# Turning sixteen pairs of gate-and-up results by DMA transposes of 16-bit halves

## The chip, the cores and the metric

The kernel runs on one core of one Trainium2 chip. The metric is the device time of one execution in microseconds (us).

## The reference

A decoder trunk of two layers on x of 512 tokens by 1024, in float32. Each layer has three parts, with a last norm behind the second layer:

```
x = x + 0.5 * swiglu(rms_norm(x, ffn1_norm), wg, wu, wd)      # D_FF = 2816
h = rms_norm(x, mix_norm); z = h @ w_in                       # q, k, v and three conv inputs
x = x + concat([sliding-window attention, short convolution]) @ w_out
x = x + 0.5 * swiglu(rms_norm(x, ffn2_norm), wg, wu, wd)

def swiglu(h, w_gate, w_up, w_down):
    return (jax.nn.silu(h @ w_gate) * (h @ w_up)) @ w_down
```

The change is in swiglu, of which there are four: between the product of gate and up, and the matmul with w_down.

## The kernel before

Every operand of a matmul is split into two parts, a rounded one (`h`, high) and the rest (`l`, low), and a product is three matmuls: high by high, low by high, high by low. The weights come from memory in tiles `raw` of 512 KB, which SyncE (SP) loads (`load`); some tiles are added to another by a second DMA that GpSimd (POOL) issues. ScalarE (ACT) casts a tile to `wh` and VectorE (DVE) subtracts, giving `wl` (`split`). There are three buffers each for `wh` and `wl`, and `take_split` splits two groups ahead (SPLIT_AHEAD = 2) of the group that TensorE (PE) works on.

Products of 2 x 2 blocks take seven block products in place of eight, after Strassen and Winograd; the sums of blocks have the names b11, b21, t2, t3, t1, t4, b22 (CHAINS). So a stage has seven steps, and each step two groups of 12 matmuls in `winograd2`. The class `Seven` makes the sums and their splits (`make`).

The 2816 columns of a feed-forward part are 22 columns of 128, in eleven pairs numbered 0 to 10. A list of stages says how they are worked (FIRST for the first part, INNER for the next two, LAST for the fourth):

```
FIRST = (
    ("p", 0), ("p", 1), ("d", (0,)), ("w", 2), ("d", (1,)), ("w", 4), ("w", 6), ("w", 8), ("u", 10),
    ("s", 2), ("d", (10,)), ("s", 6),
)
INNER = (
    ("p", 0), ("d", (0,)), ("w", 1), ("w", 3), ("w", 5), ("w", 7), ("w", 9), ("s", 1), ("s", 5),
    ("d", (9, 10)),
)
```

"w" with b computes gate and up for pairs b and b + 1 together (`winograd2`); what the change and the prediction call a pair is one such block of four columns. Its result lies with tokens on the partitions: four tiles `ups[t]` of 128 tokens by 512 columns. "s" with b multiplies the results of blocks b and b + 2 with w_down in seven products (`share`), and "d" does a plain product with w_down. Both need the results with columns on the partitions, so they have to be turned.

Before, `turn` does it: for each of the four columns c, four PE transposes of 128 x 128 into a PSUM tile `at` (line 1050), and one ACT copy of 128 x 512 from there into `raw_a` (line 1057, for blocks that go to an "s" stage) or a split (for those that go to "d"). The turns of a block wait in the list `pending`, and `turns(step)`, which the next stage calls after each of its steps, does one after steps 0 and 1 and two after step 2. A "d" stage does one after each column. There are 19 such blocks: sixteen go to "s" (`blocks`: four in each of the four parts), the rest are block 9 of INNER, twice, and of LAST, once.

`raw_a` is read when the operands of the "s" stage are made, which begins in the last stage ahead of it (in step 0 to 3 of "u" 10 or "w" 9).

The order in which instructions stand on an engine's queue is made by a scheduler when the kernel is built, from the program's order and its own estimate of when things are ready; each engine then works its queue strictly in that order. Buffers come from pools: `g2` (14 of 2 KB a partition), `g8` (4 of 8 KB), `xf` (`form`, 14 of 4 KB).

Of the kernel before, what the change touches and what calls it, by code (L numbers as in the profile page):

```python
# [8 lines left out]
F32 = mybir.dt.float32  # L9
F32R = mybir.dt.float32r  # L10
BF16 = mybir.dt.bfloat16
I32 = mybir.dt.int32
AF = mybir.ActivationFunctionType
ALU = mybir.AluOpType

P = 128
D = 1024
S = 512
# [5 lines left out]
KC = D // P  # L24
NT = S // P
# [46 lines left out]
def trunk_kernel(  # L72
# [23 lines left out]
    nc = tc.nc  # L96
# [8 lines left out]
    def psum(tag, shape, name):  # L105
        return ps.tile(shape, F32, tag=tag, bufs={"mm": 4, "sc": 2, "aux": 2}[tag], name=name)

    def g2(name, dt=F32, shape=(P, S)):
        return work.tile(list(shape), dt, tag="g2", bufs=14, name=name)

    def g8(name, dt=F32R, shape=(P, 2, 2, S)):
        return work.tile(list(shape), dt, tag="g8", bufs=4, name=name)
# [9 lines left out]
    def form(name, dt=F32R, shape=(P, KC // 2, H)):  # L122
        return xpool.tile(list(shape), dt, tag="xf", bufs=14, name=name)
# [7 lines left out]

    zero = const.tile([P, S], BF16, name="zero")
    nc.vector.memset(zero, 0.0)
# [311 lines left out]
    class Norm:  # L445
        def __init__(self, i):
            self.i = i
            self.h = [None] * KC
            self.acc = None
            self.inv = None  # L450
            self.pairs = {}
            self.begun = set()
            self.order = range(KC)
# [319 lines left out]
    bias_f = const.tile([P, NH * P], F32, name="bias")  # L773
    bias = bias_f.bitcast(BF16).rearrange("p (h k) -> p h k", h=NH)

    def make_bias():
        di = g2("dist_i", I32, (P, 2 * P))
        nc.gpsimd.iota(di, pattern=[[-1, 2 * P]], base=P, channel_multiplier=1)
        df = g2("dist", F32, (P, 2 * P))
        nc.vector.tensor_copy(df, di)  # L780
        m0 = g2("mask0", F32, (P, 2 * P))
        m1 = g2("mask1", F32, (P, 2 * P))
        nc.vector.tensor_scalar(m0, df, 0.0, FAR, op0=ALU.is_lt, op1=ALU.mult)
        nc.vector.tensor_scalar(m1, df, float(P), FAR, op0=ALU.is_ge, op1=ALU.mult)
        nc.vector.tensor_add(m0, m0, m1)
        for h in range(NH):
            nc.vector.scalar_tensor_tensor(
                bias[:, h, :], df, -(2.0 ** -(h + 1)), m0, op0=ALU.mult, op1=ALU.add
            )
# [99 lines left out]
    def ffn(norm, stages, after=None, late=None):  # L889
# [102 lines left out]
        def winograd2(b, between=None):  # L992


            name = f"{norm.i}_{b}"
            accs = {}
            gates = [g2(f"gate_{name}_{t}") for t in range(NT)]
            ups = [None] * NT
            kept = {}

            def keep(what, u, src):
                kept[what, u] = g2(f"{what}_{name}_{u}")
                nc.scalar.copy(kept[what, u], src)

            for step, (acc, operand, start) in enumerate(CHAINS):
                norm.make(operand)
                xh, xl = norm.forms[operand]
                if start:
                    tag = {"x": "mm", "y": "sc", "w": "aux"}[acc]
                    accs[acc] = [psum(tag, [P, S], f"{acc}_{name}_{u}") for u in range(2)]  # L1010
                for h in range(2):
                    _, wh, wl = take_split()
                    stream(accs[acc], wh, wl, xh, xl, h, start)
                    for u in range(2):
                        out = accs[acc][u]
                        if h == 0:
                            continue
                        if step == 0:
                            keep("p1", u, out)
                        if step == 1:  # L1020
                            nc.vector.tensor_add(gates[u], out, kept["p1", u])
                            nc.scalar.activation(gates[u], gates[u], AF.Silu)
                        if step == 2:
                            keep("u2", u, out)
                        if step == 3:
                            keep("p7", u, out)
                        if step == 4:
                            ups[2 + u] = kept["p7", u]
                            nc.vector.tensor_sub(ups[2 + u], ups[2 + u], out)
                        if step == 5:  # L1030
                            ups[u] = kept["u2", u]
                            nc.vector.tensor_sub(ups[u], out, ups[u])
                            nc.vector.tensor_mul(ups[u], ups[u], gates[u])
                        if step == 6:
                            nc.scalar.activation(gates[2 + u], out, AF.Silu)
                            nc.vector.tensor_mul(ups[2 + u], ups[2 + u], gates[2 + u])
                turns(step)
                if not first and step < 3:
                    norm.make(CHAINS[step + 4][1])
                if between:  # L1040
                    between(step)
            if b in blocks:
                raws[b] = g8(f"raw_a_{name}", F32, (P, KC // 2, S))
            if b in few:
                raws[b] = [form(f"raw_a{n}_{name}", F32, (P, 2, S)) for n in range(2)]

            def turn(c, tag="sc"):
                tp = psum(tag, [P, S], f"at_{name}_{c}")
                for t in range(NT):
                    nc.tensor.transpose(  # L1050
                        tp[:, t * P : (t + 1) * P], ups[t][:, c * P : (c + 1) * P], ident
                    )
                if b in few:
                    nc.scalar.copy(raws[b][c // 2][:, c % 2, :], tp)
                    return
                if b in raws:
                    nc.scalar.copy(raws[b][:, c, :], tp)
                    return
                if b + c // 2 not in acts:
                    acts[b + c // 2] = [form(f"a{n}_{name}_{c}", shape=(P, 2, S)) for n in "hl"]  # L1060
                hi, lo = acts[b + c // 2]
                split(hi[:, c % 2, :], lo[:, c % 2, :], tp)

            pending.extend(lambda *tag, c=c: turn(c, *tag) for c in range(NT))

        def shared(b):
            return Seven([raws[b], raws[b + 2]], room_form, f"s_{norm.i}_{b}")

        def turns(step):

            if step < 2:
                flush()
            if step == 2:
                flush(2, "mm")

        sevens = [b for what, b in stages if what == "s"]
        blocks = [b + j for what, b in stages if what in "se" for j in (0, 2)]
        few = [b + 4 for what, b in stages if what == "e"]
        raws = {}
        pending = []  # L1080

        def flush(n=1, *tag):
            for _ in range(n):
                if pending:
                    pending.pop(0)(*tag)
# [78 lines left out]
    class Finale:  # L1164
# [7 lines left out]
        def step(self, step):  # L1172


            if step > 2:
                return
            for t, tag in (((0, "sc"),), ((1, "sc"),), ((2, "mm"), (3, "aux")))[step]:
                tps = []
                for half in range(2):
                    tp = psum(tag, [P, S], f"yt_{t}_{half}")  # L1180
                    for j in range(NT):
                        nc.tensor.transpose(
                            tp[:, j * P : (j + 1) * P],
                            xs[half * NT + j][:, t * P : (t + 1) * P],
                            ident,
                        )
                    tps.append(tp)
                if t == 0:
                    self.y.append([bias_f[:, half * S : (half + 1) * S] for half in range(2)])
                if t == 1:  # L1190
                    self.y.append([g2(f"ytok{t}_{half}") for half in range(2)])
                if t > 1:
                    self.late.append(tps)
                else:
                    for half in range(2):
                        nc.scalar.copy(self.y[t][half], tps[half])
            if step == 2:
                for t, tps in zip((2, 3), self.late):
                    room = xpool.tile([P, 2, S], F32, tag=f"x{t}", name=f"ytok{t}")
                    self.y.append([room[:, half, :] for half in range(2)])  # L1200
                    for half in range(2):
                        nc.scalar.copy(self.y[t][half], tps[half])
# [387 lines left out]
```

## Time and profile before

| | |
|---|---|
| Time, median of 3 runs | 1678.52 us (1678.2 to 1678.73) |
| Profiled execution | 1678.83 us, its span 1677.0 us |
| Instructions of PE (matmuls) | 8396 |
| Busy: PE, PE weight load, DVE, ACT, POOL | 99%, 84%, 83%, 58%, 13% |
| Granted clock of PE | 0.999 |
| DMA | 285.15 MB, mean 170 GB/s |

Busy time is the share of the span in which an engine works on an instruction; matmuls are pipelined, so the busy time of PE says when it is not idle, not how much it could do. In groups by line, the columns are the line, engine, operation, what is written from what, the number, and busy time with the mean ns of one. In a timeline they are the start in us, the time taken, and the instruction, and in brackets how long the engine was idle ahead of it and who ended that.

### The profile page before, as it was taken

What the parts mean: (1) busy time and instruction counts of PE and PEld (TensorE: products, weight loads), DVE (VectorE), ACT (ScalarE), POOL (GpSimd) and SP (SyncE); (2) the same over time, 40 slices, a digit from 0 to 9 for tenths busy, and PEclk for the clock granted to TensorE, in tenths of its full rate; (3) what the DMA queues carried; (4) which work ended last, traced back from release to release, by engine and by line L of the source; (5) the groups of instructions that cost most, each with busy time, mean ns of one, the idle gap of its engine ahead of it and who ended that gap; (6) DMA issues with size and microseconds to landing.
All of it is one profiled execution on the core that took longest, in us unless ns stands there. A gap on an engine that the chain in (4) does not pass through costs nothing.

```text
span 1677.0 us, 22346 instructions
## 1 busy us (share of the span) xinstructions
PE 1668.1 (99%) x8396; PEld 1414.0 (84%) x8396; DVE 1388.3 (83%) x1824; ACT 979.6 (58%) x1361; POOL 211.2 (13%) x188
## 2 busy tenths in 40 slices
PE   9999999999999999999999999999999999999998
PEld 7888889988898888888888888888888988888886
DVE  7987679988899976799798677997788998667997
ACT  6445565466566655575465555654565766556655
POOL 0011111001211111111011111110012111111121
PEclk9999999999999999999999999999999999999999
DMA  8467777731497777778567777785125967777892
GB/s 252 99 177 189 188 195 186 188 98 51 113 228 175 177 187 185 183 197 204 173 139 179 187 187 188 189 209 167 51 64 130 233 140 194 185 187 179 224 252 74
DMA packets 192545, 285.15 MB, mean 170 GB/s; under 512 B 9068, under 2 KB 77748, under 8 KB 192436
## 3 DMA queue, kind: packets, MB, share of 16 engines
q1 hardware_dynamic: 151844, 201.26, 38.1%
q0 software_dynamic: 39872, 81.80, 28.6%
q8 instruction: 66, 1.08, 0.3%
q10 hardware_dynamic: 720, 0.66, 0.1%
q14 instruction: 43, 0.35, 0.1%
HBM read 262.71 MB, written 2.10 MB: 158 GB/s over the span
## 4 chain that ended last, share of the span: by engine, by line
PE 96%; issue 1%; DMA 1%; DVE 1%; ACT 0%; POOL 0%; SPq 0%; POOLq 0%; DVEq 0%; ACTq 0%
PE x L813 25%; PE y L813 12%; PE acc L308 8%; PE acc L309 8%; PE acc L311 7%; PE x_s L813 6%; PE w L813 6%; PE y_s L813 3%; PE x_s L798 3%; PE at L1050 2%; PE x_m L798 2%; PE w_s L813 2%; PE y_s L798 1%; PE x_e L813 1%; PE y_m L798 1%; PE acc L693 1%
## 5 line engine op out<-in xcount | busy, mean ns | idle before, releaser
L213 ACT CAST wh<-raw 128x1024 fp32r<-128x1024 f32 (+1 forms) x491 | 513.0, 1045 | 535.8 <-PE x L813 129.1
L214 DVE TENSOR_TENSOR wl<-raw,wh 128x1024 fp32r<-128x1024 f32 (+1 forms) x491 | 598.3, 1221 | 202.8 <-ACT wh L213 201.2
L308 PE MATMUL acc<-xh,wh 128*128 128x512 f32 x424 | 165.8, 392 | 0.0
L309 PE MATMUL acc<-xl,wh 128*128 128x512 f32 x424 | 165.5, 390 | 0.0
L311 PE MATMUL acc<-xh,wl 128*128 128x512 f32 x416 | 162.3, 390 | 0.0
L208 POOL DMA_DIRECT2D raw<-in_ffn_wu_dram x39 | 48.9, 1254 | 419.7 <-DMA raw<-in_ffn_wu_dram 340.2
L309 PEld LDWEIGHTS acc<-xl,wh 128*128 128x128 f32 x424 | 79.7, 188 | 15.9 <-DVE xl L489 0.2
L308 PEld LDWEIGHTS acc<-xh,wh 128*128 128x128 f32 x424 | 79.8, 188 | 15.6
L311 PEld LDWEIGHTS acc<-xh,wl 128*128 128x128 f32 x416 | 78.1, 188 | 16.4
L208 POOL DMA_DIRECT2D raw<-in_ffn_wg_dram x39 | 48.0, 1255 | 221.1 <-DMA raw<-in_ffn_wu_dram 84.1
L208 POOL DMA_DIRECT2D raw<-in_ffn_wd_dram x34 | 41.0, 1207 | 259.4 <-DMA raw<-in_ffn_wd_dram 112.0
L249 DVE TENSOR_TENSOR raw<-raw,raw 128x1024 f32<-128x1024 f32 x56 | 68.0, 1219 | 2.4 <-DMA raw<-in_ffn_wu_dram 1.7
L813 PE MATMUL w<-wh,fb21h 128*128 128x512 f32 x152 | 60.7, 399 | 0.0
L813 PE MATMUL x<-wh,ft2h 128*128 128x512 f32 x152 | 60.6, 398 | 0.0
L813 PE MATMUL y<-wh,ft3h 128*128 128x512 f32 x152 | 60.4, 398 | 0.0
L813 PE MATMUL w<-wl,fb21h 128*128 128x512 f32 x152 | 59.4, 391 | 0.0
L813 PE MATMUL x<-wl,ft2h 128*128 128x512 f32 x152 | 59.3, 390 | 0.0
L813 PE MATMUL y<-wh,ft3l 128*128 128x512 f32 x152 | 59.2, 390 | 0.0
L813 PE MATMUL y<-wl,ft3h 128*128 128x512 f32 x152 | 59.2, 390 | 0.0
L813 PE MATMUL w<-wh,fb21l 128*128 128x512 f32 x152 | 59.2, 389 | 0.0
L813 PE MATMUL x<-wl,fb11h 128*128 128x512 f32 x152 | 59.2, 389 | 0.0
L813 PE MATMUL x<-wh,ft1l 128*128 128x512 f32 x152 | 59.1, 389 | 0.0
(602 smaller groups left out, 4586.4 us busy)
## 6 DMA issues: line engine op xcount, KB each, us to landing
raw<-in_ffn_wu_dram SPq DMA_DIRECT2D x126, 512.0 KB, 4.4
raw<-in_ffn_wd_dram SPq DMA_DIRECT2D x105, 512.0 KB, 5.7
raw<-in_ffn_wg_dram SPq DMA_DIRECT2D x86, 512.0 KB, 4.7
raw<-in_ffn_wu_dram POOLq DMA_DIRECT2D x39, 512.0 KB, 8.1
raw<-in_ffn_wg_dram POOLq DMA_DIRECT2D x39, 512.0 KB, 6.2
raw<-in_w_in_dram SPq DMA_DIRECT2D x36, 512.0 KB, 3.6
raw<-in_ffn_wd_dram POOLq DMA_DIRECT2D x34, 512.0 KB, 9.0
raw<-raw POOLq DMA_DIRECT2D x21, 512.0 KB, 8.3
```

Source lines behind the costliest of these rows:

```text
L208: nc.gpsimd.dma_start(out=r, in_=rows_of(*more), accum_op=ALU.add)
L213: nc.scalar.copy(hi, raw)
L214: eng.tensor_sub(lo, raw, f32(hi))
L249: nc.vector.tensor_add(a11, a11, s1)
L308: nc.tensor.matmul(acc, hi[:, k, :], rhs[k][0], start=k == first, stop=False)
L309: nc.tensor.matmul(acc, hi[:, k, :], rhs[k][1], start=False, stop=False)
L311: nc.tensor.matmul(acc, lo[:, k, :], rhs[k][0], start=False, stop=k == last)
L693: nc.tensor.matmul(opening[n], (lo if part == "w" else hi)[:, k, :], xl if part == "x" else xh, start=n not in begun, stop=k == KC - 1 and ...
L798: nc.tensor.matmul(accs[c // 2][:, c % 2, :], w[:, k, cols], x_[:, 2 * h + k, :], start=start and c % 2 == 0 and h + k + i == 0, stop=h + ...
L813: nc.tensor.matmul(accs[u], x_[:, 2 * h + k, tok], w[:, k, :], start=start and h + k + i == 0, stop=h + k == 2 and i == 2, skip_group_chec ...
L1050: nc.tensor.transpose(tp[:, t * P : (t + 1) * P], ups[t][:, c * P : (c + 1) * P], ident)
```

## The change

Sixteen blocks (all in `blocks`) are no longer turned by PE. When such a block is done, an object `Crossing` is queued, and `turns(step)` of the next stage calls its `step` after each step. In steps 0 to 3, ACT copies one tile `ups[t]`, seen as pairs of 16-bit words, into a tile `halves`: all first words, then all second words. SP then issues a DMA transpose of these 16-bit elements into a tile `turned`, 128 x 1024 elements (256 KB). In steps 5 and 6, ACT puts the halves of a column together again in `raw_a`, two columns in each step, with a copy of 1,024 16-bit elements a partition each.

The last block of each part (8 in FIRST, 7 in the others) is `late`: everything is one step later, `turned` is two tiles from another pool, there are two DMA transposes of half the size for each tile, and step 6 puts all four columns together in eight copies of 512 elements. The three blocks that are not in `blocks` are turned by PE as before.

In the built program, PE has 256 matmul instructions (its transposes count as such) fewer, 8140; ACT has 980 copies in place of 900; SP has 80 DMA transposes (48 of 256 KB and 32 of 128 KB) beside the same 399 other DMAs; POOL's and DVE's counts don't change. On ACT, the copies that put together mostly stand behind two `wh` casts after the last `halves` and ahead of the next.

```diff
             if b in blocks:
-                raws[b] = g8(f"raw_a_{name}", F32, (P, KC // 2, S))
+                crossing.append(Crossing(b, name, ups))
+                return
...
-                if b in raws:
-                    nc.scalar.copy(raws[b][:, c, :], tp)
-                    return
...
+        class Crossing:
+            def __init__(self, b, name, ups):
+                self.b, self.name, self.ups = b, name, ups
+                self.late = int(b == max(blocks))
+                self.to = None
+
+            def words(self, ap):
+                return ap.bitcast(U16).rearrange("p (n two) -> p two n", two=2)
+
+            def step(self, step):
+                t = step - self.late
+                if t == 0 and self.late:
+                    self.to = [form(f"turned{n}_{self.name}", U16, (P, NT, S)) for n in range(2)]
+                elif t == 0:
+                    self.to = g8(f"turned_{self.name}", U16, (P, 2, NT, S))
+                if 0 <= t < NT:
+                    halves = g2(f"halves{t}_{self.name}", U16, (P, 2, S))
+                    nc.scalar.copy(halves, self.words(self.ups[t]))
+                    tok = slice(t * P, (t + 1) * P)
+                    if self.late:
+                        for n in range(2):
+                            nc.sync.dma_start_transpose(self.to[n][:, :, tok], halves[:, n, :])
+                    else:
+                        nc.sync.dma_start_transpose(
+                            self.to.rearrange("p a c s -> p (a c) s")[:, :, tok],
+                            halves.rearrange("p a n -> p (a n)"),
+                        )
+                if step == 5 + self.late:
+                    raws[self.b] = g8(f"raw_a_{self.name}", F32, (P, KC // 2, S))
+                due = {6: (0, 1, 2, 3)} if self.late else {5: (0, 1), 6: (2, 3)}
+                for c in due.get(step, ()):
+                    to = self.words(raws[self.b][:, c, :])
+                    if self.late:
+                        for n in range(2):
+                            nc.scalar.copy(to[:, n, :], self.to[n][:, c, :])
+                    else:
+                        nc.scalar.copy(to, self.to[:, :, c, :])
+                return step == 6
...
                 flush(2, "mm")
-
+            if crossing and crossing[0].step(step):
+                crossing.pop(0)
+
+        crossing = []
```

More of the change, by code (lines that the diff above doesn't have):

```diff
@@ L11 @@
 BF16 = mybir.dt.bfloat16
+U16 = mybir.dt.uint16
 I32 = mybir.dt.int32
```

## The prediction

> **What bounds the kernel.** I read the page first: busy time, slices, chain. Its lines:
>
> ```profile
> PE 1668.1 (99%) x8396; PEld 1414.0 (84%) x8396; DVE 1388.3 (83%) x1824; ACT 979.6 (58%) x1361; POOL 211.2 (13%) x188
> DMA  8467777731497777778567777785125967777892
> PE 96%; issue 1%; DMA 1%; DVE 1%; ACT 0%; POOL 0%; SPq 0%; POOLq 0%; DVEq 0%; ACTq 0%
> ```
>
> The chain that ends last is TensorE (PE) for 96% of the span. Next, the list of PE's waits, which is complete in two lines:
>
> ```profile
> PE idle L138 <- DVE warm L640: 1.2, 1, 1.2
> PE x_e L813 <- DVE bias L1206: 0.2, 1, 0.2
> ```
>
> PE never waits for a result in the body of the kernel. So an instruction taken from PE is time gained, as long as everything that feeds PE stays ahead of it; and whatever falls behind now shows at once, because no PE idle time exists to hide it. All other engines have room on average, DMA least (the digits are 7 in most slices, 8 and 9 in some).
>
> The profiled execution took 1678.83 us: its span of 1677.0 and 1.83 around it. The median of the runs is 1678.52, 0.31 less. A change under 0.2% (3.4 us) can't be told from none.
>
> **What PE loses.** The 256 transposes of the sixteen pairs go. What they cost is not their busy time, since matmuls overlap; it is read from two stages with the same 168 matmuls, first one without turns, then one with the 16 transposes of a pair. The timeline gives the first matmul of three stages that follow each other, the windows the counts:
>
> ```profile
> 117.20 0.39 PE L813 MATMUL x<-wh,fb11h 128*128 128x512 f32 x1
> 155.28 0.39 PE L813 MATMUL x<-wh,fb11h 128*128 128x512 f32 x1
> 195.24 0.39 PE L813 MATMUL x<-wh,fb11h 128*128 128x512 f32 x1
> 117.20:155.28 38.08, 38.08 (x169) 31.54 (x168) 27.53 (x29) 19.62 (x24) 4.02 (x4) 1.00 0.61 166
> 155.28:195.24 39.96, 39.96 (x186) 33.14 (x185) 27.79 (x29) 22.05 (x29) 3.58 (x4) 1.00 0.74 185
> ```
>
> The columns after the window's length are busy time and count of PE, PEld, DVE, ACT and POOL, then granted clock (1.00), DMA share and GB/s. 39.96 - 38.08 = 1.88 us for a pair, and 16 x 1.88 = 30.1 us. With everything else hidden the profiled time becomes 1678.8 - 30.1 = 1648.7 us.
>
> **What ScalarE (ACT) gets.** The groups that matter, by line:
>
> ```profile
> L1050 PE MATMUL at<-ident,u 128*128 128x128 f32 x152 | 28.9, 271 | 0.0
> L1050 PE MATMUL at<-ident,p 128*128 128x128 f32 x152 | 29.2, 273 | 0.0
> L1057 ACT COPY raw_a<-at 128x512 f32<-128x512 f32 x64 | 35.8, 586 | 3.1 <-PE at L1050 3.0
> L213 ACT CAST wh<-raw 128x1024 fp32r<-128x1024 f32 (+1 forms) x491 | 513.0, 1045 | 535.8 <-PE x L813 129.1 <-issue 93.4 <-PE y L813 84.2
> L214 DVE TENSOR_TENSOR wl<-raw,wh 128x1024 fp32r<-128x1024 f32 (+1 forms) x491 | 598.3, 1221 | 202.8 <-ACT wh L213 201.2
> ```
>
> The 304 transposes of L1050 are 19 pairs; 48 stay, for the pairs that don't cross. ACT loses all 64 copies of L1057 (0.59 us each, 37.5 in all). It gets 64 copies that lay halves apart (1,024 16-bit elements a partition), and for putting together 48 of 1,024 elements (twelve pairs) and 32 of 512 (the four late pairs). No row shows a 16-bit copy with strides. By elements it is the cast of 1,024 (1.05 us) and the copy of 512 (0.59); by bytes half of that; were the stride to cost twice, 2.1 and 1.2. I take the elements: 64 x 1.05 + 48 x 1.05 + 32 x 0.59 = 136.5, less 37.5 is 99 us more, ACT from 980 to 1079 us, 65% of 1650. In the stage with turns above: 22.05 - 4 x 0.59 + 8 x 1.05 = 28.1 of 38.08, so it fits. At twice the price it would be 36.5 of 38.08: no room for any wait, and the gain would be gone.
>
> The groups also say what ACT must not hold up: each group of matmuls needs a cast wh (ACT) and behind it the rest wl (DVE, VectorE), and ACT works strictly in order. DVE's own instructions stay the same in number; some move by a group or two.
>
> **What waits, and how much it may wait.** The new chain of a pair is: the fourth laying apart on ACT (after step 3 of the next stage), a DMA transpose on SP, then the putting together on ACT, which waits for all four transposes. In the changed program's order this stands on ACT after two more wh casts, in step 5, and ahead of the next one. Behind the waiting copy on ACT stand wh, then wl on DVE, then PE. The stage from 117.20 on shows the room. Rows of ACT, DVE, PE, SP's queue and POOL:
>
> ```profile
> 139.89 0.58 ACT L1003 COPY p<-y 128x512 f32<-128x512 f32 x1
> 141.66 1.05 ACT L213 CAST wh<-raw 128x1024 fp32r<-128x1024 f32 x1 [1.19 <-PE x L813]
> 144.38 1.05 ACT L213 CAST wh<-raw 128x1024 fp32r<-128x1024 f32 x1 [1.67 <-PE x L813]
> 147.10 1.05 ACT L213 CAST wh<-raw 128x1024 fp32r<-128x1024 f32 x1 [1.67 <-PE y L813]
> 148.18 1.23 DVE L214 TENSOR_TENSOR wl<-raw,wh 128x1024 fp32r<-128x1024 f32 x1 [1.49 <-ACT wh L213]
> 152.56 0.39 PE L813 MATMUL x<-wh,fb22h 128*128 128x512 f32 x1
> 141.28 0.37 SPq L196 DMA_DIRECT2D raw<-in_ffn_wg_dram  x1
> 140.16 1.20 POOL L208 DMA_DIRECT2D raw<-in_ffn_wu_dram  x1 [28.27 <-DMA raw<-in_ffn_wu_dram]
> 142.63 1.20 POOL L208 DMA_DIRECT2D raw<-in_ffn_wu_dram  x1 [1.28 <-DMA raw<-in_ffn_wu_dram]
> ```
>
> Laying apart follows the copy at 139.89: it runs from 140.47 to 141.52, and the transpose is issued then. The wh of 147.10 gives the wl that ends at 149.41; PE takes that group at 152.56. Slack: 3.15 us. So that wh may start at 150.25, and two copies of putting together (2.1 us) may start at 148.15 without PE noticing. The transpose has 148.15 - 141.52 = 6.6 us to land. Each microsecond beyond holds PE by about a microsecond, and at 6.6 + 1.88 = 8.5 us the pair has given back all it gained.
>
> How long it takes, no row shows. The rows that bound it are issues, with size and median time to landing, and the DMA engines in that stretch:
>
> ```profile
> out_dram<-ytok SPq DMA_DIRECT2D x5, 256.0 KB, 2.2
> raw<-in_ffn_wu_dram SPq DMA_DIRECT2D x126, 512.0 KB, 4.4
> raw<-in_ffn_wu_dram POOLq DMA_DIRECT2D x39, 512.0 KB, 8.1
> raw<-raw POOLq DMA_DIRECT2D x21, 512.0 KB, 8.3
> 142.00:147.00 5.00, 5.00 (x24) 4.14 (x23) 3.73 (x4) 1.77 (x2) 1.20 (x1) 1.00 1.01 210
> 147.00:151.00 4.00, 4.00 (x20) 3.30 (x19) 2.78 (x4) 2.11 (x2) 0.00 (x0) 1.00 1.09 268
> ```
>
> A transpose moves 256 KB. The best is the plain store of that size, 2.2 us; the worst a copy inside SBUF of twice the size, 8.3, behind the load that SP issued just ahead at 141.28, 4.4: 12.7 us. The low end is unlikely, since the DMA engines are full (1.01 and 1.09) just then, with the two adding loads that POOL issued at 140.16 and 142.63. I take the middle, 7.5 us: 0.85 us too late, for each of the sixteen pairs 13.6 us of PE time.
>
> The Trainium skill (DMA: Bandwidth & Descriptors, Latency and other measured facts) gives 261 GB/s for a DMA transpose, by which 256 KB would be an estimated 1.0 us of transfer. By it the transpose would land inside the 6.6 us, and the sum would be the 1648.7 of everything hidden; no run here shows a transpose yet.
>
> SP's own time costs nothing that I can see: 80 more issues stand on a queue that mostly waits for raw buffers to come free:
>
> ```profile
> SPq L196 <- DVE wl L214: 1072.1, 298, 22.3
> 155.26 1.06 ACT L213 CAST wh<-raw 128x1024 fp32r<-128x1024 f32 x1 [0.54 <-PE x L813]
> ```
>
> A load behind a transpose is delayed with it. The load issued at 141.28 is first read by the cast at 155.26: 14.0 us, of which landing takes 4.4. So 9 us are free; a transpose that held SP's queue for longer than that would cost PE the excess.
>
> **The four late pairs** cross beside the splits of the next stage's operands. ACT and DVE there:
>
> ```profile
> 235.00:257.00 22.00, 22.00 (x186) 21.96 (x185) 20.96 (x25) 15.50 (x24) 3.34 (x4) 1.00 0.73 172
> 257.00:268.00 11.00, 11.00 (x94) 11.00 (x93) 11.00 (x14) 7.30 (x9) 2.74 (x3) 1.00 0.86 161
> 699.70:739.50 39.80, 39.80 (x185) 33.06 (x184) 36.41 (x37) 27.60 (x34) 3.62 (x3) 1.00 0.73 185
> ```
>
> In the first (one pair), ACT gets 4 x 1.05 + 8 x 0.59 - 4 x 0.59 = 6.6 us: 22.1 us in 22.0 - 1.88 = 20.1. Two microseconds don't fit and go into the next window, where ACT has 3.7 free but DVE none. I put 1.0 us on PE. In the third (three such stages), 34.2 of 37.9: it fits, and DVE has 36.41 of 37.9. Nothing added.
>
> **The sum**: 30.1 - 13.6 - 1.0 = 15.5 us gained; 1678.8 - 15.5 = 1663.3, against the median 1663.
>
> **Rivals.**
>
> All hidden: the transposes land within 6.6 us. For it: T moves half of what a load moves, and loads land in 4.4. Against it: the full DMA engines. Time 1649, or 1650 with the 1.0 us of the late pair.
>
> Transposes wait for the adding loads: a transpose that is counted as landed only with what POOL's queue had going lands when the load issued at 142.63 does, 142.63 + 8.1 = 150.7, that is 9.2 us after issue. Stall 2.6 x 16 = 41.6 against 30.1: 1690. Against it: SP's plain loads land in 4.4 beside the same traffic, as a median. The Trainium skill (DMA: Bandwidth & Descriptors, Queues, rings and completion order) says that a DMA's semaphore increment lands only after every earlier write of that DMA engine, across its queues; by that rule this rival is the outcome, and the 4.4 us of the loads don't speak for it.
>
> Transposes slow in themselves: behind half a load and as slow as the copy inside SBUF, 2.2 + 8.3 = 10.5 us. Stall 3.9 x 16 = 62.4: 1711. It decides from 8.5 us on, at the copy that puts together, in step 5 of each stage. At the worst bound, 12.7, it is 1746.
>
> No change: landing at 8.5 us, or ACT's strided copies at twice the price: 1678.
>
> ACT and DVE overrun: copies and late pairs cost more than their elements say, a little beyond break-even; 1683.
>
> **How the numbers follow.** Chances: forecast 0.40, with its own range from 1655 to 1672 (landing 7.1 to 8.1 us); all hidden 0.20; waiting for adding loads 0.15; slow transposes 0.13; no change 0.07; overrun 0.05. Faster 0.60, same 0.07, slower 0.33. The range goes from 1648 (all hidden) to 1711 (slow transposes); beyond it lie the slower half of the slow case and a little below, together under 0.15.
>
> **What would show it.** PE with 8,140 matmuls; stages after the first down to 38.1 us plus the stall. In ACT's waits a new line, the copy raw_a waiting for the DMA of turned: this is my 0.85 us a pair, in step 5. In the DMA issues a transposing line with its time to landing: under 6.6 us the first rival, over 8.5 the slower ones. PE's waits, empty now, should name wh or wl, about 14 us in all. The copies halves and raw_a near 1.05 us. I am wrong if PE waits stay empty, or if loads (raw) become what ACT waits for, or if a copy takes much over 1.05 us.

## The result and the profile after

The changed kernel takes 1747.37 us (median of 4 runs), against 1678.38 before on the same chip: a ratio of 1.0389, 95% interval 1.0305 to 1.0474. By that ratio it is slower by 65 us where 15.5 were to be gained. The profiled execution took 1756.95 us, its span 1755.2. The run at 1778.9, over 1.5% above the fastest and at a lower clock (0.970), is left out of the ratio, and nothing on record shows what made it longer. The other three differ by 20 us (1736.53 to 1756.95), where the kernel before differs by 0.5.

The page after: busy time, granted clock and DMA in 40 slices, and the chain that ended last.

```profile
PE 1669.5 (95%) x8140; PEld 1398.9 (80%) x8140; DVE 1378.0 (79%) x1824; ACT 1077.2 (61%) x1441; POOL 212.2 (12%) x188
PEclk9999998999999999999999999999999999999899
DMA  8478997741397789998567999894127778889992
PE 4%; DVE 2%; issue 1%; ACT 0%; DMA 0%; DVEq 0%; ACTq 0%
```

PE has the 8,140 matmuls that were announced, and is no longer busy throughout. Its list of waits, which had 1.4 us in all before, is headed by the casts, and ACT's list shows why the casts are late (columns: total, times, longest):

```profile
PE x L814 <- ACT wh L214: 61.0, 11, 8.4
PE w_s L799 <- ACT wh L214: 8.5, 1, 8.5
```

```profile
ACT raw_a L1106 <- DMA turned<-halves: 77.6, 12, 12.3
ACT raw_a L1104 <- DMA turned<-halves: 28.4, 4, 10.8
```

All sixteen pairs wait at the copy that puts together: the twelve early ones at L1106, the four late ones at L1104. The tile `turned`, its instructions (minimum, median, maximum in ns) and its time to landing:

```profile
L1093 SPq DMA_TRANSPOSE turned<-halves x48: 1231/1232/2934, 123.3 to 1578.7; - x48
L1106 ACT COPY raw_a<-turned x48: 1312/1338/1357, 152.8 to 1596.2; 128x1024 uint16<-128x1024 uint16 x48
L1104 ACT COPY raw_a<-turned x32: 743/760/784, 274.4 to 1647.6; 128x512 uint16<-128x512 uint16 x32
DMA to landing us min/median/max: 2.5/5.3/15.8
```

The median, 5.3 us, is under the 6.6 that the prediction allowed; but a pair needs all four transposes, and the fourth is not a median one. The stage that the prediction walked through, in the timeline of POOL, SP's queue and ACT:

```profile
138.93 1.19 POOL L209 DMA_DIRECT2D raw<-in_ffn_wu_dram  x1 [25.40 <-DMA raw<-in_ffn_wu_dram]
141.41 1.20 POOL L209 DMA_DIRECT2D raw<-in_ffn_wu_dram  x1 [1.29 <-DMA raw<-in_ffn_wu_dram]
139.95 1.45 SPq L1093 DMA_TRANSPOSE turned<-halves  x1
152.77 2.51 ACT L1106 COPY raw_a<-turned 128x1024 uint16<-128x1024 uint16 x2 [9.13 <-DMA turned<-halves]
```

The fourth transpose takes 12.8 us. What it does to PE shows in windows of the same stage (after the length: PE, PEld, DVE, ACT, POOL; then granted clock, DMA share, GB/s):

```profile
142.60:148.05 5.45, 5.45 (x25) 4.51 (x24) 2.09 (x3) 1.04 (x1) 0.02 (x1) 1.00 1.21 180
150.55:156.24 5.69, 0.39 (x2) 0.00 (x1) 0.02 (x1) 3.47 (x4) 0.00 (x0) 0.84 0.90 220
156.24:161.40 5.16, 5.12 (x11) 3.60 (x12) 5.13 (x7) 4.73 (x5) 1.20 (x1) 0.51 0.57 145
161.40:166.90 5.50, 5.50 (x26) 4.53 (x25) 5.50 (x7) 3.19 (x4) 1.20 (x1) 1.00 1.00 165
```

PE stands for 5.3 us and then runs at half the clock for 5.2 more: 11 matmuls in place of some 24. The Trainium skill (TensorE: Matmul & The Clock Gate, Part 1) says that about 3.4 us of idleness halve the clock and about as much work restores it; here it is 5.3 and 5.2, and experiment 2 shows that less idleness can do it too. So this stall costs its own length and, at a clock of 0.51 for 5.16 us, an estimated 2.5 us behind it. Over the run the mean granted clock fell from 0.999 to 0.978.

Where the 78 us of span went, by the length of stages (first matmul to first matmul, some of 26; "early start" and "late pairs too" are experiments 5 and 9 below):

| stage, by its start before | before | changed | early start | late pairs too |
|---|---|---|---|---|
| 117.20, pair 2 crosses | 38.08 | 46.22 | 38.27 | 38.08 |
| 155.28, pair 4 | 39.95 | 48.65 | 38.08 | 38.08 |
| 195.24, pair 6 | 39.93 | 38.35 | 38.08 | 38.08 |
| 257.0, after late pair 8 (to 308.3) | 51.23 | 62.63 | 51.23 | 51.23 |
| 699.7, late pair 7 | 39.93 | 49.00 | 39.93 | 38.08 |
| 914.2, early | 39.93 | 38.08 | 38.08 | 38.08 |

(Pair 2 was turned in the stage before 117.20, which is now 2.03 us shorter.) Summed over all stages, those of early pairs are 39.5 us longer than before and those of late pairs 38.8. Some stages gain their 1.85 in full, others lose 6 to 9. The question is what decides that.

### The profile page after: what moved, and what is told of

It is laid out like the page before. It is cut to its first block, busy times and chain, and to the rows that moved or that the text cites. A ratio compares the mean times of both kernels' runs of the same rounds, so it can differ in the third digit from the quotient of the medians.

```text
span 1755.2 us, 22158 instructions
## 1 busy us (share of the span) xinstructions
PE 1669.5 (95%) x8140; PEld 1398.9 (80%) x8140; DVE 1378.0 (79%) x1824; ACT 1077.2 (61%) x1441; POOL 212.2 (12%) x188
## 3 DMA queue, kind: packets, MB, share of 16 engines
q8 instruction: 64, 1.05, 0.3%
## 5 line engine op out<-in xcount | busy, mean ns | idle before, releaser
L814 PE MATMUL x<-wh,fb22h 128*128 128x512 f32 x152 | 68.3, 450 | 61.0 <-ACT wh L214 61.0
L1106 ACT COPY raw_a<-turned 128x1024 uint16<-128x1024 uint16 x48 | 61.1, 1337 | 77.6 <-DMA turned<-halves 77.6
L209 POOL DMA_DIRECT2D raw<-in_ffn_wu_dram x39 | 48.9, 1254 | 405.1 <-DMA raw<-in_ffn_wu_dram 258.2
L310 PEld LDWEIGHTS acc<-xl,wh 128*128 128x128 f32 x424 | 79.7, 188 | 15.9 <-DVE xl L490 0.2
L814 PEld LDWEIGHTS x<-wh,fb22h 128*128 128x128 f32 x152 | 32.9, 216 | 71.6 <-ACT wh L214 65.7
L209 POOL DMA_DIRECT2D raw<-in_ffn_wg_dram x39 | 48.1, 1242 | 280.2 <-DMA raw<-in_ffn_wu_dram 101.6
L209 POOL DMA_DIRECT2D raw<-in_ffn_wd_dram x34 | 41.0, 1215 | 278.2 <-DMA raw<-in_ffn_wd_dram 115.3
L814 PE MATMUL x<-wl,fb22h 128*128 128x512 f32 x152 | 67.3, 443 | 1.9 <-DVE wl L215 1.5
L814 PE MATMUL x<-wh,fb22l 128*128 128x512 f32 x152 | 66.1, 435 | 0.0
L814 PE MATMUL x<-wh,fb11l 128*128 128x512 f32 x152 | 59.4, 391 | 0.0
L814 PE MATMUL x<-wh,fb11h 128*128 128x512 f32 x152 | 59.4, 391 | 0.0
```

The source lines that it names most:

```text
L209: nc.gpsimd.dma_start(out=r, in_=rows_of(*more), accum_op=ALU.add)
L310: nc.tensor.matmul(acc, hi[:, k, :], rhs[k][1], start=False, stop=False)
L814: nc.tensor.matmul(accs[u], x_[:, 2 * h + k, tok], w[:, k, :], start=start and h + k + i == 0, stop=h + k == 2 and i == 2, skip_group_chec ...
L1106: nc.scalar.copy(to, self.to[:, :, c, :])
```

## The experiments

Theories at the start. A: transposes run slowly where POOL's adding loads run beside them. B: any transfer of 256 KB in that place is as late. C: ACT's copies, longer than costed, are the cause. D: the rival of the prediction, transposes count as landed only behind the adding loads. Line numbers in experiments shift by a few.

**1. Plain copies in place of transposes**, 1,024 pieces of 256 bytes as before. The transposition itself is left out.

```diff
-  nc.sync.dma_start_transpose(to[(a c), tok], halves)
+  nc.sync.dma_start(to[:, (a c), tok], halves as p (a c) q)
```

> Each of the 80 DMA transposes is replaced by a plain DMA from halves to turned with the same 256 KB (or 128 KB), the same pieces of 256 bytes, the same place on SP's queue; the transposition itself is left out, so turned holds the words in their old order. Everything else is the changed kernel. Theory A (transposes run beside the adding loads of POOL's queue crawl, a plain copy does not): the fourth transfer lands in 4 to 7 us, ACT's wait for turned falls from 106 us to under 20, time 1650 to 1665. Theory B (any 256 KB transfer there comes as late, since the DMA engines are full): 1735 to 1757 as in the changed kernel. Theory C (ACT's strided copies of 1.34 and 0.76 us are what overruns): no change either, 1735 to 1757.

1681.51 us, ratio 1.0016 [0.9988, 1.0044]; ten runs from 1668 to 1698. Neither A nor B has its number. The transposition matters, but of the twelve early pairs nine are hidden wholly or in part and three lose 4 to 5.5 us each. One of the three, timeline, landing and waits:

```profile
939.75 1.20 POOL L209 DMA_DIRECT2D raw<-in_ffn_wu_dram  x1 [18.53 <-DMA raw<-in_ffn_wu_dram]
940.32 0.60 SPq L1093 DMA_DIRECT2D turned<-halves  x1
```

```profile
DMA to landing us min/median/max: 11.4/11.4/11.4
```

```profile
ACT raw_a L1106 <- DMA turned<-halves: 48.8, 12, 8.0
```

This copy, issued 0.57 us behind an adding load, takes 11.4 us, and it transposes nothing. That pointed back to the changed kernel, where the fourth transposes fall into two groups. One of the good ones, with its adding load:

```profile
974.15 1.23 SPq L1093 DMA_TRANSPOSE turned<-halves  x1
974.40 1.20 POOL L209 DMA_DIRECT2D raw<-in_ffn_wu_dram  x1 [19.68 <-DMA raw<-in_ffn_wu_dram]
```

```profile
DMA to landing us min/median/max: 4.7/4.7/4.7
```

Ten of the twelve early pairs' fourth transposes have a landing in the trace. Five were issued from 0.5 us ahead of to 0.2 us behind the first adding load, and landed in 4.7 to 8.1 us; five were issued 0.4 to 1.4 us behind it, and took 12.3 to 15.9. Who comes first is a race of less than a microsecond. Adding loads are slow to begin: from 138.9 to 142.9, POOL's queue, which issued at 138.93, has no packet yet (in eleven such stages of this trace the first packet comes 1.9 to 5.5 us behind the issue).

```profile
q1 hardware_dynamic: 444, 0.88, 86.2%
```

(q1 is SP's queue, q0 POOL's; packets, MB, share of 16 engines.) A transpose that is through by then meets none of them. The packets bear the two groups out: where POOL's first packet is in the trace, the quick transposes had fewer than 80 of their 1,024 pieces still to move when it came, the slow ones 998 or more.

For plain copies the order alone doesn't decide: issued 0.2 to 0.6 us behind, two took 7.2 and 7.8 us and three 11.2 to 11.6.

**2. POOL's transfers write in place of adding.** The edit changes the 120 loads of line L209, which leaves out the sums of weights; the other 36 of the 156 DMAs that POOL issues still add.

```diff
-  nc.gpsimd.dma_start(out=r, in_=rows_of(*more), accum_op=ALU.add)
+  nc.gpsimd.dma_start(out=r, in_=rows_of(*more))
```

> The changed kernel with its transposes, but POOL's 156 adding loads write instead of add (same bytes, queue, places; the sums of weights are left out). Theory A in its narrow form (it takes an adding transfer ahead of a transpose to make it crawl): transposes land in 3 to 7 us everywhere, 1650 to 1665. Theory A in its wide form (any transfer of POOL's queue beside a transpose does it) and theory C: 1735 to 1757.

1739.02 us, 1.0341 [1.0285, 1.0397]. Early pairs' landings go up to 11.3 us, so it is not the adding of these loads; the narrow form of A falls:

```profile
DMA to landing us min/median/max: 2.7/5.4/11.3
```

This run also shows shorter stalls of PE. Windows of one of 2.03 us and of the 4 us behind it, where the clock is 0.70 (there, another wait of 0.53 us follows):

```profile
1113.81:1115.84 2.03, 0.01 (x1) 0.01 (x1) 0.03 (x1) 1.72 (x3) 0.00 (x0) 1.00 1.04 406
1115.84:1119.84 4.00, 3.47 (x9) 2.51 (x10) 4.00 (x6) 4.00 (x7) 0.72 (x1) 0.70 0.43 112
```

That isn't so for every stall of this length. In all the traces here, each stall of PE of 2.6 us or more is followed by a clock of 0.50 to 0.75 in the next 4 us (the shortest, 2.63 us in this run, by 0.64). Of the seven between 2.0 and 2.4 us, three are (2.03, 2.06 and 2.12 in this run), and four keep a clock of 1.00 (2.00 here, 2.30 in experiment 7, 2.27 and 2.35 in experiment 8).

**3. Two tiles laid apart in each step.**

> Two tiles are laid apart in a step rather than one, so the fourth transpose is issued two steps (about 10 us) earlier, ahead of the first adding load of its stage; everything else as in the changed kernel. Theories A, B and D (transposes count as landed only behind the adding loads): the fourth transpose lands in 3 to 6 us, before it is needed, PE's stalls of 75 us go but for some tenths in the steps where ACT now has two copies one behind the other: 1650 to 1665. Theory C (ACT's copies are too long): no better than 1730.

1688.84 us, 1.0066 [1.0045, 1.0086]. A miss: no early pair's transpose takes longer than 7.6 us any more, and still ACT waits:

```profile
ACT raw_a L1106 <- DMA turned<-halves: 25.4, 8, 3.4
```

In the built program the scheduler, which thinks the transposes landed sooner, had moved the copies that put together two steps up as well. There they wait 3 us again, with casts behind them.

**4. Transposes that nobody reads**; PE turns as before.

> PE turns the sixteen pairs as in the kernel before, and in addition the halves are laid apart and transposed by DMA as in the changed kernel, but nobody reads the transposed tiles: no copy on ACT waits for them. If only ACT's wait for the late transpose costs time: 1678 to 1685. If the crawl also makes the loads of weights late enough to stop PE: 1695 to 1730, with PE waiting for wh behind raw.

1703.76 us, 1.0156 [1.0138, 1.0174]. Without any wait for `turned` there is a cost of 25 us. Part of it is that loads come late; before, this line had 4.4 us:

```profile
ACT wh L214 <- DMA raw<-in_ffn_wg_dram: 31.6, 11, 6.3
```

**5. Start a step earlier, put together in the program's order, late pairs by PE.**

```diff
-  t = step - self.late
+  t = step + 1                      # first tile in step 6 of its own stage
-  due = {6: (0, 1, 2, 3)} if self.late else {5: (0, 1), 6: (2, 3)}
+  due = {4: (0,), 5: (1, 2), 6: (3,)}
-  nc.scalar.copy(to, ...)
+  tc.keep_in_program_order(nc.scalar.copy(to, ...))
```

> Only the twelve early pairs cross by DMA; the four late ones are turned by PE as in the kernel before. Each crossing starts one step earlier (first tile in step 6 of its own stage, the fourth in step 2 of the next, some 4 us ahead of POOL's first adding load), and the copies that put together are pinned in the program's order: one after step 4, two after step 5, one after step 6. Theory A (a transpose crawls only when POOL's transfers run between its packets, and the late pairs cost ACT time of their own): no wait of ACT for turned, PE without waits there, 12 x 1.85 us gained of 1678.4: 1656, up to 1664 with tenths of a microsecond lost in some stages. If transposes cost time in some other way (loads of weights late, SP's queue), it is no better than 1675.

1659.1 us, 0.9884 [0.9869, 0.9899]: faster than both kernels. PE's waits are the whole list again, and the longest landing is 7.7:

```profile
PE idle L139 <- DVE warm L641: 1.2, 1, 1.2
PE xt L660 <- DMA xin<-in_x_dram: 1.1, 1, 1.1
PE acc L309 <- DVE x L1203: 1.0, 2, 0.6
PE x_e L814 <- DVE bias L1258: 0.2, 1, 0.2
```

```profile
DMA to landing us min/median/max: 2.7/5.3/7.7
```

The copies are as long as in the changed kernel (1.36 us), so theory C falls.

**6. The changed kernel, late pairs by PE.**

> The changed kernel, but its four late pairs are turned by PE as in the kernel before; the twelve early pairs as changed. If the late pairs' copies and waits at the entry of the product with w_down cost what the stages show (11.4, 1.4, 1.0 and 0.7 us longer than before, some of it in the last stage ahead too), the time falls by about 15 us and the stalls of the early pairs stay: 1715 to 1740. If the late pairs are the main loss, it comes under 1700.

1725.29 us, 1.0297 [1.0269, 1.0325]: most of the loss stays, and it is the early pairs'. The late pairs' share is uncertain, since the runs of either kernel differ by 20 us and more: 15 us by the ratios, and 38.8 by the stages of the one execution above.

**7. Transposes from ACT's queue.**

> The changed kernel with its 80 transposes issued from ACT's queue in place of SP's, so that they run on another hardware queue beside SP's loads in every step. If any second queue beside a transpose makes it crawl, the first three transposes of a pair take 8 us or more too, and the time goes above 1760. If only POOL's transfers do, the first three land in 2.5 to 6 us as before and the fourth in 10 to 16; time near 1757, more for ACT's issuing time.

1766.03 us, 1.0522 [1.0479, 1.0565]. Neither expectation came out. The first three transposes of an early pair land in 2.7 to 10.3 us beside SP's loads, later than from SP's queue. Of the ten fourth ones with a landing in the trace only one is slow, issued 0.12 us behind the first adding load; the other nine land in 5.3 to 8.5:

```profile
DMA to landing us min/median/max: 2.7/6.7/16.5
```

So a second hardware queue makes transposes later, but only beside POOL's loads did one take over 11 us. This kernel is slow mostly for another reason: the three later stages in which a late pair crosses are 15 to 17 us longer than before. ACT now spends 1.25 us on issuing each transpose; that this is the cause was not tested.

**8. Put together 12 us later, transposes in the changed place, late pairs by PE.**

> Twelve early pairs cross, the late four are turned by PE. The halves are laid apart and the transposes issued in steps 0 to 3 as in the changed kernel, so the fourth still meets POOL's adding loads; but the four copies that put together are pinned after step 6, some 12 us later than in the changed kernel, and behind them stands one cast. If the stalls were only ACT's wait for a late transpose, nobody waits now: 1656 to 1664, as with transposes issued ahead of the adding loads. If slow transposes also hold the loads of weights that run beside them (they landed 12 to 15 us after issue in the slow stages, against 9 us to spare), time is lost still, with ACT's casts waiting for raw: 1668 to 1700.

1670.13 us, 0.9945 [0.9932, 0.9958], 11 us above experiment 5, though almost nothing waits for `turned`. The waits that are new:

```profile
ACT raw_a L1111 <- DMA turned<-halves: 2.4, 2, 1.4
DVE raw L250 <- DMA raw<-in_ffn_wu_dram: 16.6, 7, 4.6
PE w L814 <- DVE wl L215: 6.2, 3, 2.4
```

So up to 11 us of what the collision costs come through the loads of weights that are held up with it; this is argued from these waits, as the two kernels also differ in when the transposes are issued. Experiment 6 differs from this one only in where the copies stand on ACT: about 55 us came through ACT's wait.

**Theory E.** The queues take turns packet by packet. DMA queues in three windows: the changed kernel from 1487 to 1490 (loads against adding loads), experiment 1 from 944 to 946 (a plain copy against adding loads), the changed kernel from 147 to 150 (a transpose against adding loads):

```profile
q0 software_dynamic: 186, 0.38, 69.1%
q1 hardware_dynamic: 183, 0.37, 38.1%
```

```profile
q0 software_dynamic: 158, 0.32, 87.9%
q1 hardware_dynamic: 138, 0.09, 23.8%
```

```profile
q1 hardware_dynamic: 232, 0.07, 90.0%
q0 software_dynamic: 56, 0.11, 35.0%
```

In the first, 186 packets stand against 183: one for one; in the second, 158 against 138, nearly so. The Trainium skill (DMA: Bandwidth & Descriptors, Queues, rings and completion order) says that a DMA engine goes round its queues packet by packet; these two windows agree. A POOL packet takes 69.1% x 48 / 186 = 0.178 us (16 engines for 3 us are 48), and a tile cut into 1,024 pieces of 256 bytes needs 64 turns on each of 16 engines: an estimated 64 x 0.178 = 11.4 us if POOL's queue always has a packet ready, during which the tile's queue hardly moves bytes.

The third window is not of that kind: 232 packets against 56 is four to one, and the packets of both queues are slow, 90.0% x 48 / 232 = 0.186 us for a transpose's and 35.0% x 48 / 56 = 0.30 us for POOL's. Nor are the 12.8 us of this transpose made of turns: its first packet comes at 144.8, 4.8 us behind its issue, after the loads ahead of it on SP's queue, and from 145 to 147 some 730 of its 1,024 pieces pass. So theory E fits plain copies; what slows a transpose beside POOL's loads is another thing, and it is open.

**10. Plain copies in pieces of 1 KB**, 256 packets a tile. The transposition is left out here too.

> As the experiment with plain copies (the transposition is left out, same 256 KB, same place on SP's queue), but in pieces of 1 KB rather than 256 bytes: 256 packets a tile in place of 1,024. Theory E, new after the first seven runs: POOL's queue and SP's queue take turns on the DMA engines packet by packet; a POOL packet of 2 KB takes 0.18 us, so a tile of 1,024 small packets, 64 for each of 16 engines, needs 64 x 0.2 = 12.8 us when it falls behind the adding loads, and one of 256 packets a quarter of that. By E the fourth tile lands in 3 to 8 us in every stage, behind the adding loads too, ACT's wait for turned in the early pairs stays under 15 us, and all twelve early pairs gain: 1665 to 1674, the late pairs' loss staying. If any transfer behind the adding loads is as late, whatever its pieces, 1678 to 1700 with landings of 11 us as in that experiment.

1668.92 us, 0.9948 [0.9931, 0.9965]. A copy behind an adding load by 0.3 us, as late as some that took 11 us with small pieces:

```profile
687.68 1.20 POOL L209 DMA_DIRECT2D raw<-in_ffn_wu_dram  x1 [21.48 <-DMA raw<-in_ffn_wu_dram]
688.00 0.61 SPq L1093 DMA_DIRECT2D turned<-halves  x1
```

```profile
DMA to landing us min/median/max: 2.6/2.6/2.6
```

But this copy takes no turns with the adding load. From 688 to 690 POOL's queue has no packet:

```profile
q1 hardware_dynamic: 307, 0.37, 53.9%
```

Its first one comes at 690.0, when 236 of the copy's 256 are through: no load stands just ahead of the copy on SP's queue here, where in experiment 1 one was issued 0.46 us ahead of it. Nine other pairs' fourth copies land in 2.4 to 3.0 us. The one that moved among the adding load's packets, issued at 140.26 and 0.8 us behind, took 8.7 us, the longest of the run and a little over E's 8. So the time is in E's range, but for E itself this run has one copy only. The waits are not as expected, 52.1 us in 38 of up to 5.7, since ACT's order came out differently here (a column no longer needs all four tiles). The run speaks against D: the copy landed at 690.6, and the adding load issued ahead of it only at 694.6.

**11. The changed kernel without the adding loads** of L209, so without the sums of weights.

> The changed kernel with its DMA transposes, but POOL's adding loads are left out (the sums of weights are missing). By theory E nothing takes turns with the transposes: they land in 2.5 to 7 us everywhere, the early pairs gain, the late pairs keep what of their loss is ACT's and DVE's time: 1655 to 1675. If transposes crawl beside SP's own loads of weights, waits of 10 us and more stay: over 1700.

1671.72 us, 0.9962 [0.9947, 0.9976]. The early pairs' transposes land in 2.7 to 7.9 us, the long landings are gone; some 70 of the changed kernel's microseconds hang on its meeting with POOL's loads. (This kernel also moves 63 MB less, but experiment 5 moves them all and has no long landing either.) What is left above 1650 is mostly the late pairs: their stages are 11.5 us longer than before.

**The late pairs.** In the changed kernel the eight copies of the first one stand between ACT's casts at the entry of the product with w_down. The first of them and the first cast behind them, in ACT's timeline:

```profile
274.36 1.40 ACT L1104 COPY raw_a<-turned 128x512 uint16<-128x512 uint16 x2 [6.08 <-DMA turned<-halves]
282.80 1.99 ACT L214 CAST wh<-raw 128x1024 fp32r<-128x1024 f32 x2
```

Six us of waiting and eight copies pass without a `wh`. That step of PE takes 14.4 us in the changed kernel (first line), 5.8 before (second line):

```profile
269.50:283.90 14.40, 5.93 (x51) 5.72 (x49) 8.15 (x11) 9.54 (x16) 2.41 (x2) 0.77 0.94 191
257.00:262.80 5.80, 5.80 (x51) 5.80 (x50) 5.80 (x8) 5.20 (x7) 0.97 (x1) 1.00 0.96 171
```

Is it ACT's load or only the place?

**9. Three of the four late pairs cross as in experiment 5.**

> The kernel with the crossing one step earlier and pinned copies, and in addition the three late pairs of the second, third and fourth part cross in the same way (two transposes a tile, eight copies); only the first part's late pair stays with PE. If the early start is enough for them too: 3 x 1.85 us below the 1659 of that kernel, 1653 to 1655. If ACT, which gets some 8 us more in these stages beside 27.6 of 40, or DVE, whose room there is 1.5 us, can't take it: 1660 to 1675, PE waiting for wh or for the operands' splits at the entry of the product with w_down.

1652.66 us, 0.9846 [0.9832, 0.9859], the best of all, five runs within 2.9 us. Two stages that lost before, late pair and the one after it:

```profile
688.28:726.36 38.08, 38.08 (x170) 31.53 (x168) 33.98 (x35) 32.41 (x40) 4.82 (x4) 1.00 0.96 219
726.36:764.44 38.08, 38.08 (x170) 31.53 (x168) 37.83 (x38) 27.40 (x33) 6.62 (x6) 1.00 0.87 217
```

Place, not load, for these three. All fifteen pairs give their 1.85 us: 15 x 1.85 = 27.8, and the span went from 1677.0 to 1649.2. The first part's late pair, beside steps of half the length, was not tried in this way.

## Why the prediction was wrong

Right: PE's gain for a pair (1.88 us predicted, 1.85 measured where nothing waits); the place (step 5, ACT's copy, casts queued behind it, then DVE, then PE); the slack of 6.6 us; that SP's own time costs nothing (experiments 5 and 9 have 48 and 72 transposes on that queue, and PE waits for no load of weights).

Wrong, by its terms:

- **Landing of the fourth transpose, 7.5 us taken as the middle of 2.2 and 12.7.** It is not one number but two: 4.7 to 8.1 when it is ahead of POOL's adding loads, 12.3 to 15.9 when behind; the mean of the ten seen is 10.2. The step that failed was to lay one median into a fork. The rows of the order were there, POOL's issues at 140.16 and 142.63 beside an issue of the transpose at 141.5, that is behind the first one; none showed yet what this order costs. The worst bound, 12.7, met that stage's 12.8 by luck, as it was added up from a copy and a load, and was too low for others. (The range from 1655 to 1672 belongs, by its own sum, to landings of about 7.0 to 8.0 us rather than 7.1 to 8.1; nothing hangs on that.)
- **"Each microsecond beyond holds PE by about a microsecond."** Too little: behind a long stall PE runs at half the clock for some microseconds, an estimated 2.5 us more in the stage at 115.4, where the landing was 6.2 late and the stage 8.1 longer. Where the clock stayed at 1.00 it was too little as well: landings of 7.7 and 8.1 us, 1.1 and 1.5 late, made the stages at 642.6 and 683.4 longer than 38.08 by 2.7 and 3.2.
- **The four late pairs, 1.0 us.** With the other three stages "nothing added", they were to be 6.5 us shorter in all; without POOL's loads of L209 (experiment 11) they are 11.5 longer. Their busy times fitted; that eight copies stand in order ahead of the casts was not counted.
- **Copies with strides.** Laying apart 1.04, as taken; putting together 1.34 and 0.76 in place of 1.05 and 0.59. That is 0.29 and 0.17 us a copy, hidden in experiments 5 and 9.

Of the rivals, "transposes slow in themselves" has the nearest times (1711, worst 1746), with the wrong cause: the first one of a pair, far from POOL's loads, mostly lands in 2.7 to 2.9 us. "Transposes wait for the adding loads" named the right partner, but not the way: the transpose at 139.95 landed at 152.75, 3.7 us ahead of the second adding load (156.5). The estimate from the Trainium skill's 261 GB/s (DMA: Bandwidth & Descriptors, Latency and other measured facts), 1.0 us, is for the transfer alone and fits no landing: the quickest transposes of 256 KB need 2.7 us from issue to landing.

Shown is who has to be beside a transpose to make it slow: without POOL's loads (experiment 11) or ahead of them (experiments 3 and 5) none of the early pairs' takes over 8 us. Open is how: why the packets of both queues are slow then, 0.186 us for a transpose's 256 bytes and 0.30 for POOL's 2 KB, where a plain copy of the same pieces takes its turns. Plain pieces behind adding loads took up to 11.6 us.

## What to carry to other kernels

Cost a DMA by what runs beside it at its place: here the same transpose landed in 5 to 8 us ahead of another queue's transfers and in 12 to 16 behind them, and a median landing hid that. Issue it ahead of the other queue's transfers, and pin whatever waits for it far enough down an in-order engine, because a scheduler that thinks it fast will move the wait up. A long stall of PE costs more than its length: here the clock dropped behind each one of 2.6 us or more.

## What was not expected of the hardware

In the changed kernel an order of issue that differs by less than 0.4 us parts landings of 5 to 8 us from those of 12 to 16; the times of equal runs differ by 20 us with that race in the kernel and by 3 without it (experiments 9 and 11). The adding loads' first packets come 1.9 to 5.5 us behind their issue (142.9 against 138.93 in one stage). Issuing a DMA transpose holds SP's queue for 1.23 us, a plain DMA of the same pieces 0.60.
